# Three chunk loads of 16 rows a partition become two loads of 24 rows in a row-softmax kernel

## Chip, cores and metric

The kernel runs on one core of a Trainium2 chip. The metric is the device time of one execution in microseconds, the median of several runs.

## What is computed

A softmax with temperature 0.5 over the last dimension of a float32 tensor of shape (16, 1024, 512), that is 16384 rows of 512 values:

```python
x_scaled = x / 0.5
x_max = np.max(x_scaled, axis=-1, keepdims=True)
exp_x = np.exp(x_scaled - x_max)
out = exp_x / np.sum(exp_x, axis=-1, keepdims=True)
```

Each row is on its own. Input and output are 33.55 MB each.

## The kernel before

**Tiling.** The rows are cut into C = 8 chunks of 128 x 16 rows, numbered 0 to 7 here (the change's "fourth to sixth" are chunks 3, 4 and 5). In a chunk each of the 128 partitions holds G = 16 rows that lie one after the other in HBM, so a partition's share is one run of 16 x 512 x 4 bytes = 32 KiB. `LOADS` (L38) says how a chunk's rows are split over DMAs: chunk 0 in 4 and 12 rows, chunks 1 to 6 whole, chunk 7 without its last row, which `load_last_row` brings later in two small DMAs of GpSimd. There are six chunk buffers (`BUFS`, L42); chunks 6 and 7 take the buffers of chunks 0 and 1 and so wait until those are stored.

**Blocks.** Work goes by blocks (`BLOCKS`, L39): chunk 0 is three blocks (4, 4 and 8 rows), chunks 1 to 6 are one block each, chunk 7 two of 8 rows. For a block

- `shift` issues the chunk's load when nobody has yet (L66, on the SP queue), takes the negated maximum of each row with one VectorE reduction (L74) and doubles it to a bias (L78);
- `exponentials` runs one ScalarE activation per row, exp(2x + bias), in place, and sums the row in the same instruction (L103);
- `scale_vector` takes reciprocals of the sums (L120) and multiplies seven eighths of the rows on VectorE (L122); `scale_scalar` multiplies the rest on ScalarE (L131);
- `store` sends the whole chunk once its last block is done (L139, on ScalarE's DMA queue, 16 rows a partition).

**Order.** The order of instructions on each engine is the order of the program text (L143 to L161); no scheduler moves them. VectorE thus alternates: scale block i, maxima of block i + 2, scale block i + 1, and so on. Each engine runs its list in order, so an instruction that waits holds up all that stands behind it on that engine. The SP queue holds the loads in the order of the chunks. The first seven load DMAs (chunks 0 to 5) wait for nothing and are issued in the first 4 us; those of chunks 6 and 7 wait for the stores of chunks 0 and 1. Stores go out through the other queue (q10 in the profile; the loads are q1). Both queues are worked off by the same 16 DMA engines.

Of the kernel before, what the change touches and what calls it, by code (L numbers as in the profile page):

```python
# [1 line left out]

# [4 lines left out]


@with_exitstack
def kernel(  # L10
    ctx: ExitStack,
    tc: tile.TileContext,
    x: bass.AP,
    out: bass.AP,
):
    nc = tc.nc
    fp32 = mybir.dt.float32
    P = nc.NUM_PARTITIONS
    AX = mybir.AxisListType.X
    EXP = mybir.ActivationFunctionType.Exp  # L20
    COPY = mybir.ActivationFunctionType.Copy
    MAX = mybir.AluOpType.max

    D = x.shape[-1]
    xf = x.flatten_outer_dims()
    of = out.flatten_outer_dims()
    N = xf.shape[0]

    G = 16
    C = N // (P * G)
    assert C * P * G == N
    xr = xf.rearrange("(c p g) d -> c p g d", p=P, g=G)
    outr = of.rearrange("(c p g) d -> c p g d", p=P, g=G)
    WHOLE = [(0, G)]
    LOADS = [[(0, 4), (4, G)]] + [WHOLE] * 6 + [[(0, G - 1)]]  # L38
    BLOCKS = [[(0, 4), (4, 8), (8, G)]] + [WHOLE] * 6 + [[(0, 8), (8, G)]]  # L39
    STORES = [WHOLE] * 8  # L40
    BMAX = 16
    BUFS = 6  # L42

    data = ctx.enter_context(tc.tile_pool(name="data", bufs=BUFS))
    stats = ctx.enter_context(tc.tile_pool(name="stats", bufs=6))

    ctx.enter_context(tc.manual_schedule())


    warm = stats.tile([P, 1], fp32, name="warm", bufs=1)  # L50
    nc.vector.memset(warm, 0.0)  # L51
    nc.scalar.activation(out=warm, in_=warm, func=EXP)  # L52

    chunks = {}
    blocks = [(c, lo, hi) for c in range(C) for lo, hi in BLOCKS[c]]
    n = len(blocks)
    biases, sums, recips = {}, {}, {}

    def load(c):
        if c < BUFS:  # L60
            chunks[c] = data.tile([P, G, D], fp32, name="xt")
        else:
            chunks[c] = chunks[c - BUFS]
        xt = chunks[c]
        for lo, hi in LOADS[c]:
            nc.sync.dma_start(out=xt[:, lo:hi, :], in_=xr[c][:, lo:hi, :])  # L66

    def shift(i):
        c, lo, hi = blocks[i]
        if c not in chunks:  # L70
            load(c)
        b = hi - lo
        negmax = stats.tile([P, BMAX], fp32, name="negmax")
        nc.vector.tensor_reduce(  # L74
            negmax[:, 0:b], chunks[c][:, lo:hi, :], axis=AX, op=MAX, negate=True
        )
        biases[i] = stats.tile([P, BMAX], fp32, name="bias")
        nc.vector.tensor_scalar_mul(biases[i][:, 0:b], negmax[:, 0:b], 2.0)  # L78

    def load_last_row(signal):
        seen = stats.tile([P, 1], fp32, name="seen", bufs=1)
        nc.gpsimd.tensor_copy(out=seen, in_=signal)  # L87
        c = C - 1
        halves = "p (h d) -> p h d"
        to = chunks[c - BUFS][:, G - 1, :].rearrange(halves, h=2)  # L90
        of_ = xr[c][:, G - 1, :].rearrange(halves, h=2)
        for p0, p1 in ((P - 2, P), (0, P - 2)):
            nc.gpsimd.dma_start(  # L93
                out=to[p0:p1], in_=of_[p0:p1], max_dma_last_dim=2 * D
            )

    def exponentials(i, rows):
        c, lo, hi = blocks[i]
        if i not in sums:
            sums[i] = stats.tile([P, BMAX], fp32, name="sums")  # L100
        for g in rows:
            row = chunks[c][:, lo + g, :]
            nc.scalar.activation(  # L103
                out=row,
                in_=row,
                func=EXP,
                bias=biases[i][:, g : g + 1],
                scale=2.0,
                accum_out=sums[i][:, g : g + 1],
            )  # L110
            if c == BUFS - 1 and g == 10:
                load_last_row(sums[i][:, g : g + 1])


    def scale_vector(i):
        c, lo, hi = blocks[i]
        b = hi - lo
        k = b - b // 8
        recips[i] = stats.tile([P, BMAX], fp32, name="recip")
        nc.vector.reciprocal(recips[i][:, 0:b], sums[i][:, 0:b])  # L120
        rows = chunks[c][:, lo : lo + k, :]
        nc.vector.tensor_mul(  # L122
            rows, rows, recips[i][:, 0:k].unsqueeze(2).broadcast_to((P, k, D))
        )

    def scale_scalar(i):
        c, lo, hi = blocks[i]
        b = hi - lo
        for g in range(b - b // 8, b):
            row = chunks[c][:, lo + g, :]  # L130
            nc.scalar.activation(  # L131
                out=row, in_=row, func=COPY, scale=recips[i][:, g : g + 1]
            )

    def store(i):
        c, _, end = blocks[i]
        for lo, hi in STORES[c]:
            if hi == end:
                nc.scalar.dma_start(  # L139
                    out=outr[c][:, lo:hi, :], in_=chunks[c][:, lo:hi, :]  # L140
                )

    shift(0)  # L143
    shift(1)

    def rows(i):
        c, lo, hi = blocks[i]
        cut = hi - lo - (2 if c == 1 else 0)
        return range(cut), range(cut, hi - lo)

    exponentials(0, rows(0)[0])
    for i in range(n):
        if i + 1 < n:
            exponentials(i + 1, rows(i + 1)[0])
        scale_vector(i)
        scale_scalar(i)
        if i + 2 < n:
            shift(i + 2)
        store(i)
        if i + 1 < n:  # L160
            exponentials(i + 1, rows(i + 1)[1])  # L161


# [1 line left out]
_INS = ['x']  # L165
_OUTS = [((16, 1024, 512), 'float32')]


# [23 lines left out]
```

## Time and profile before

The median of 3 runs is 162.08 us (161.99 to 162.23); the profiled execution has a span of 160.3 us on the core.

| engine | busy us | share of span | instructions |
|---|---|---|---|
| VectorE (DVE) | 134.6 | 84% | 45 |
| ScalarE (ACT) | 102.2 | 64% | 273 |
| GpSimd (POOL) | 1.9 | 1% | 7 |

| work | count | mean ns of one |
|---|---|---|
| row maxima of 16 rows, L74 | 6 | 8679 |
| scaling of 14 rows on VectorE, L122 | 6 | 7626 |
| exponential of one row, L103 | 128 | 708 (and 187 to read the sum) |
| load of a whole chunk, 4096 KB, L66 | 6 | 34.8 us from issue to landing (median) |
| store of a chunk, 4096 KB, L139 | 8 | 22.7 us from issue to landing (median) |

How to read it: TensorE is not used. The page's line "DMA" gives, for 40 equal slices of the span, the mean busy share of the 16 DMA engines in tenths (9 is 90% or more). Its chain is the work that ended last, followed back from the last instruction, in shares of the span. A line of the waits reads "engine and line <- what it waited for: us in total, times, longest us". A line of the timeline starts with the start and the duration in us. A line of the DMA view for a queue gives packets, MB and the time that the packets took, as a share of 16 engines over the stretch asked for; a line for an issue gives the number of issues, KB each and the median us from issue to landing. The trace also keeps each DMA packet with queue, size, start and duration.

### The profile page before, as it was taken

To read this page: it belongs to the slowest core of one execution; us is meant where nothing else is said; L and a number is where in the kernel's file an instruction comes from. 1 tells how busy PE (TensorE), PEld (TensorE's weight loads), DVE (VectorE), ACT (ScalarE), POOL (GpSimd) and SP (SyncE) were. 2 spreads that over 40 slices of the span, in tenths; PEclk is the share of its full clock that TensorE was granted. 3 is DMA by queue.
4 is the path that set the end of the run, shared out by engine and by line. 5 is a ranking of instruction groups with operands and counts; after the bars stand their busy time and mean duration, and the time that the engine had idled before them with its cause. 6 is when DMAs were issued, how large, how long until landed. Compare 5 with 4: busy or idle time off the path is not lost.

```text
span 160.3 us, 410 instructions
## 1 busy us (share of the span) xinstructions
DVE 134.6 (84%) x45; ACT 102.2 (64%) x273; POOL 1.9 (1%) x7
## 2 busy tenths in 40 slices
DVE  0608999999999999999999999999999999957000
ACT  3071549069989963998199909991899891790000
POOL 0000000000000000000000000030000000000000
DMA  5999999999999999999999989999999999999993
GB/s 180 474 393 523 393 393 507 409 393 452 458 393 401 393 393 515 401 393 491 425 393 466 450 385 470 415 422 462 421 437 401 450 458 401 425 474 401 401 507 139
DMA packets 2578, 67.13 MB, mean 419 GB/s; under 512 B 328, under 2 KB 328, under 8 KB 400
## 3 DMA queue, kind: packets, MB, share of 16 engines
q1 hardware_dynamic: 1296, 33.29, 49.1%
q10 hardware_dynamic: 1152, 33.55, 48.5%
q0 software_dynamic: 128, 0.26, 0.4%
q14 instruction: 2, 0.02, 0.0%
HBM read 33.55 MB, written 33.55 MB: 419 GB/s over the span
## 4 chain that ended last, share of the span: by engine, by line
DVE 75%; DMA 7%; issue 5%; ACT 3%; SPq 0%
DVE negmax L74 42%; DVE xt L122 32%; DMA xt<-in_x_dram 7%; ACT xt L103 3%; DVE bias L78 1%; DVE recip L120 1%; SPq L66 0%
## 5 line engine op out<-in xcount | busy, mean ns | idle before, releaser
L103 ACT ACTIVATE xt<-xt,bias 128x512 f32<-128x512 f32 x128 | 90.4, 708 | 41.4 <-DVE bias L78 40.5
L74 DVE TENSOR_REDUCE negmax<-xt 128x16 f32<-128x8192 f32 (+2 forms) x11 | 69.9, 6352 | 9.4 <-DMA xt<-in_x_dram 9.4
L122 DVE TENSOR_TENSOR xt<-xt,recip 128x7168 f32<-128x7168 f32 (+2 forms) x11 | 62.0, 5637 | 0.4
L103 ACT ACTIVATION_READ_ACCUMULATOR xt<-xt,bias 128x1 f32 x128 | 23.9, 187 | 0.0
L131 ACT ACTIVATE xt<-xt,recip 128x512 f32<-128x512 f32 x15 | 9.9, 706 | 0.0
L120 DVE RECIPROCAL recip<-sums 128x16 f32<-128x16 f32 (+2 forms) x11 | 2.4, 218 | 1.8 <-ACT xt L103 1.8
L78 DVE TENSOR_SCALAR bias<-negmax 128x16 f32<-128x16 f32 (+2 forms) x11 | 1.9, 173 | 0.4
L52 ACT ACT_TABLE_LOAD x1 | 1.3, 1283 | 0.7 <-PEq L176 0.7
L93 POOL DMA_DIRECT2D xt<-in_x_dram x2 | 1.5, 741 | 0.5 <-issue 0.5
L87 POOL COPY seen<-sums 128x1 f32<-128x1 f32 x1 | 0.2, 183 | 103.6 <-ACT xt L103 103.6
L51 DVE MEMSET warm<- 128x1 f32 x1 | 0.1, 59 | 0.8 <-PEq L176 0.8
L52 ACT ACTIVATE warm<-warm 128x1 f32<-128x1 f32 x1 | 0.2, 203 | 0.0
L176 POOL MEMSET const-float32-0.0<- 128x1 f32 x1 | 0.1, 93 | 0.2 <-issue 0.2
L176 POOL MEMSET const-bfloat16-1.0<- 128x1 bf16 x1 | 0.1, 95 | 0.0
L176 POOL MEMSET const-uint8-127<- 128x1 uint8 x1 | 0.1, 95 | 0.0
L176 POOL MEMSET const-float32-1.0<- 128x1 f32 x1 | 0.1, 93 | 0.0
## 6 DMA issues: line engine op xcount, KB each, us to landing
out_dram<-xt ACTq DMA_DIRECT2D x8, 4096.0 KB, 22.7
xt<-in_x_dram SPq DMA_DIRECT2D x6, 4096.0 KB, 34.8
xt<-in_x_dram SPq DMA_DIRECT2D x1, 3840.0 KB, 28.1
xt<-in_x_dram SPq DMA_DIRECT2D x1, 3072.0 KB, 11.5
xt<-in_x_dram SPq DMA_DIRECT2D x1, 1024.0 KB, 4.7
xt<-in_x_dram POOLq DMA_DIRECT2D x1, 252.0 KB, 15.2
xt<-in_x_dram POOLq DMA_DIRECT2D x1, 4.0 KB, 8.7
```

What stands on the lines that cost most here:

```text
L51: nc.vector.memset(warm, 0.0)
L52: nc.scalar.activation(out=warm, in_=warm, func=EXP)
L74: nc.vector.tensor_reduce(negmax[:, 0:b], chunks[c][:, lo:hi, :], axis=AX, op=MAX, negate=True)
L78: nc.vector.tensor_scalar_mul(biases[i][:, 0:b], negmax[:, 0:b], 2.0)
L87: nc.gpsimd.tensor_copy(out=seen, in_=signal)
L93: nc.gpsimd.dma_start(out=to[p0:p1], in_=of_[p0:p1], max_dma_last_dim=2 * D)
L103: nc.scalar.activation(out=row, in_=row, func=EXP, bias=biases[i][:, g : g + 1], scale=2.0, accum_out=sums[i][:, g : g + 1],)
L120: nc.vector.reciprocal(recips[i][:, 0:b], sums[i][:, 0:b])
L122: nc.vector.tensor_mul(rows, rows, recips[i][:, 0:k].unsqueeze(2).broadcast_to((P, k, D)))
L131: nc.scalar.activation(out=row, in_=row, func=COPY, scale=recips[i][:, g : g + 1])
L176: nc = _bacc.Bacc("TRN2", target_bir_lowering=False, num_devices=1)
```

## The change

Chunks 3, 4 and 5 become one group of 48 rows a partition. They lie in one buffer of three times the size, and in HBM a partition now owns 48 consecutive rows (96 KiB) of the group's 6144, where before it owned three separate runs of 16. The group is loaded by two DMAs of 24 rows each, so a partition's run per DMA is 48 KiB instead of 32 KiB, and there are two DMAs and two landings instead of three. A load is issued as far as the rows of the wanted chunk need it: before chunk 3's maxima the first, before chunk 4's the second, before chunk 5's none. The maxima of chunk 3 wait for the first load; those of chunk 4 take rows 16 to 31 and so wait for both; those of chunk 5 need nothing more. The aim is larger pieces for the DMA engines and fewer transfers.

Blocks, computing instructions, their order on each engine, and the stores (still one of 16 rows a partition for each chunk, 32 KiB pieces) are as before; a store's pieces for chunks 3 to 5 now lie 96 KiB apart in HBM instead of side by side. The buffers take the same memory.

```diff
+    GROUPS = [(0,), (1,), (2,), (3, 4, 5), (6,), (7,)]
-    WHOLE = [(0, G)]
-    LOADS = [[(0, 4), (4, G)]] + [WHOLE] * 6 + [[(0, G - 1)]]
-    STORES = [WHOLE] * 8
+    LOADS = [
+        [(0, 4), (4, G)],
+        [(0, G)],
+        [(0, G)],
+        [(0, 24), (24, 48)],
+        [(0, G)],
+        [(0, G - 1)],
+    ]
...
+    chunks, group_of, waiting = {}, {}, {}
+    for k, members in enumerate(GROUPS):
+        first, m = members[0], len(members)
+        hbm = slice(first * P * G, (first + m) * P * G)
+        into = xf[hbm].rearrange("(p g) d -> p g d", p=P)
+        back = of[hbm].rearrange("(p g) d -> p g d", p=P)
+        if first < BUFS:
+            xt = data.tile([P, m * G, D], fp32, name=f"xt{k}")
+        else:
+            xt = group_of[first - BUFS][0]
+        for at, c in enumerate(members):
+            group_of[c] = (xt, into, back, k, at * G)
+            chunks[c] = xt[:, at * G : (at + 1) * G, :]
+        waiting[k] = list(LOADS[k])
...
     def load(c):
-        xt = chunks[c]
-        for lo, hi in LOADS[c]:
-            nc.sync.dma_start(out=xt[:, lo:hi, :], in_=xr[c][:, lo:hi, :])
+        xt, into, _, k, at = group_of[c]
+        while waiting[k] and waiting[k][0][0] < at + G:
+            lo, hi = waiting[k].pop(0)
+            nc.sync.dma_start(out=xt[:, lo:hi, :], in_=into[:, lo:hi, :])
```

## The prediction

> Chunks are numbered 0 to 7. The two new loads are A (rows 0 to 23 of the long partition runs: all of chunk 3, half of chunk 4) and B (rows 24 to 47: the rest of chunk 4, all of chunk 5). Times in the trace are from the span's start; the measured time, 162.08 us, is 1.8 us more than the span.
>
> **What bounds the kernel now.** I read the page first: its slices and its chain.
>
> ```profile
> DMA  5999999999999999999999989999999999999993
> DMA packets 2578, 67.13 MB, mean 419 GB/s; under 512 B 328, under 2 KB 328, under 8 KB 400
> q1 hardware_dynamic: 1296, 33.29, 49.1%
> q10 hardware_dynamic: 1152, 33.55, 48.5%
> DVE 75%; DMA 7%; issue 5%; ACT 3%; SPq 0%
> ```
>
> Two things are full at once. The 16 DMA engines are busy from the first slice to the last: loads (q1) and stores (q10) take 97.6% of their time. And the chain that ended last is VectorE. The waits say how much air VectorE has:
>
> ```profile
> DVE negmax L74 <- DMA xt<-in_x_dram: 9.4, 2, 4.8
> DVE recip L120 <- ACT xt L103: 1.8, 1, 1.8
> ```
>
> It waits twice for chunk 0 at the start, once for ScalarE at the end, and nowhere between: from 12.7 to 141.4 us it runs without a gap, so a delay there goes through to its end undiminished. The timeline at the end shows how the two limits meet:
>
> ```profile
> 143.44 3.89 DVE L122 TENSOR_TENSOR xt<-xt,recip 128x3584 f32<-128x3584 f32 x1
> 147.42 0.34 ACTq L139 DMA_DIRECT2D out_dram<-xt  x1
> ```
>
> The last store is issued at 147.42 us. In the packet records its first pieces start at 148.63 to 148.98 us on most engines, at once after the store before it, so the engines don't idle. The first load needed 1.02 us from issue (0.74) to its first piece (1.76), so this store could have started at about 148.44. VectorE's tail therefore has 0.2 to 0.5 us of slack against the DMA engines; I take 0.3.
>
> Then the loads that change, by asking the DMA view for one issue each (chunks 3, 4 and 5, issued at 2.76, 3.26 and 3.79 us; they land at 42.3, 57.3 and 76.7 us), and what VectorE needs them for:
>
> ```profile
> xt<-in_x_dram SPq DMA_DIRECT2D x1, 4096.0 KB, 39.6
> ```
> ```profile
> xt<-in_x_dram SPq DMA_DIRECT2D x1, 4096.0 KB, 54.1
> ```
> ```profile
> xt<-in_x_dram SPq DMA_DIRECT2D x1, 4096.0 KB, 72.9
> ```
> ```profile
> 53.94 8.68 DVE L74 TENSOR_REDUCE negmax<-xt 128x16 f32<-128x8192 f32 x1
> 63.02 7.62 DVE L122 TENSOR_TENSOR xt<-xt,recip 128x7168 f32<-128x7168 f32 x1
> 70.56 8.68 DVE L74 TENSOR_REDUCE negmax<-xt 128x16 f32<-128x8192 f32 x1
> ```
>
> The maxima of chunk 3 start at 53.94, of chunk 4 at 70.56, of chunk 5 at 87.18 us. Before the change the slack is 11.6, 13.2 and 10.5 us. Chunk 4's is the one to watch: it will need B as well.
>
> Last, how loads and stores share the engines. From 17 to 41 us only loads run; from 58 to 66 us both do:
>
> ```profile
> q1 hardware_dynamic: 347, 10.32, 99.7%
> ```
> ```profile
> q10 hardware_dynamic: 50, 1.64, 47.4%
> q1 hardware_dynamic: 49, 1.61, 46.4%
> ```
>
> 10.32 MB are 315 pieces of 32 KiB: 0.997 x 16 x 24 / 315 = 1.215 us each. With both queues filled the pieces alternate one for one. The packet records give 0.309, 0.912, 1.138 and 1.213 us for pieces of 8, 24, 30 and 32 KiB: 0.0368 ns a byte plus 7.5 ns, hence an estimated 1.816 us for 48 KiB.
>
> **What the Trainium skill says.** "DMA: Bandwidth & Descriptors", section "Queues, rings and completion order": an engine takes its queues in turn, packet by packet. The trace agrees (49 against 50). Same page, "Why a DMA increments its semaphore by 16 and not by 1": 128 partitions are spread over 16 engines, each engine's last descriptor is its part of the signal, one descriptor moves one contiguous run, and only the full 16 means landed. The trace agrees: 9 loads left 1296 packets, which is 9 x (128 + 16), and the slowest engine sets a landing (chunk 4: fifteen engines by 55.96, the last at 57.34). Its "Where 436 GB/s comes from" puts the ceiling at 435 GB/s; here 32 KiB in 1.213 us on 16 engines is 432. Bigger pieces can't go past it.
>
> **The change part by part.** *Removed:* 128 of 384 load pieces and one DMA. 128 x 7.5 ns / 16 = 0.06 us of engine time, and one of nine signals. Bytes, engines' instructions and stores are the same. VectorE, ScalarE and GpSimd keep their order; ScalarE's wait for B moves into the middle of chunk 4's exponentials, behind VectorE's own wait for it. SP issues two DMAs for three within its first 4 us, hidden behind chunk 0's load. These cost nothing.
>
> *Chunk 3 waits for A.* A starts where chunk 3's load did: chunk 2's pieces end at 31.4 to 31.7 us in the records. 8 pieces x 1.816 = 14.53, so A ends at about 46.1 and lands (0.35 us later, as the other loads do) by 46.5, some 47 on the slowest engine. Needed at 53.94: hidden by chunk 2's maxima and chunk 1's scaling.
>
> *Chunk 4 waits for B.* Only this can reach the end. B starts at about 46.1, and its 8 pieces take 14.53. Chunk 0's store, issued at 44.02, alternates with them, so the question is how many store pieces come before B's signal. In the trace of before, the piece in hand about 1.0 to 1.5 us after that issue was followed by two more load pieces before the first store piece (49.3 to 49.5 us), and the signal takes a turn of its own (the order at 54 to 56 us is: eighth load piece, store piece, signal, store piece). After the change the piece in hand is A's last; I let the two turns be A's signal and B's first piece. Then a store piece follows each of B's 8: 8 x 1.213 = 9.70. In this first meeting of the queues the load pieces also ran longer, 1.6 to 1.8 us in place of 1.213, for one or two pieces: 0.4 to 0.85 us, I take 0.6. Sum: 46.1 + 14.53 + 9.70 + 0.6 + 0.35 = 71.3 us on most engines. One engine was 0.46 us behind at chunk 3 (42.33 against 41.87); with it B lands at 71.8. The same sum for chunk 4 before, 41.3 + 9.71 + 3 x 1.213 + 0.85 + 0.35 = 55.9, meets its 55.7 to 55.96.
>
> So VectorE waits 71.8 - 70.56 = 1.2 us. Queued behind this reduce are chunk 4's bias, which ScalarE's exponentials need, the scaling of chunk 3 with its store, and all later work of VectorE; nothing takes the delay up before the last store. That is issued 1.2 us later; with 0.3 us of slack the end moves by 0.9 us. Less the 0.06: 162.08 + 0.9 = **163.0 us**. Bounds: one meeting piece fewer or more and no slack or 0.5 us of it give +0.5 to +1.6.
>
> *Later loads.* Chunk 6's load waits for chunk 0's store, which, getting 40% of the time beside 48 KiB pieces and not 50%, lands at about 71.7 instead of 68.1. q1 then stands empty for 3 to 4 us, but q10 still holds chunk 1's store, issued at 58.9, so the engines stay busy. Chunk 6 then lands at about 96 us and is needed at 105; it costs nothing.
>
> **Rivals.** (a) *The early switch goes the other way*: the two turns are B's first two pieces. One store piece fewer precedes the signal; B lands at 71.8 - 1.2 = 70.6 if the lagging engine follows suit, 71.0 if it meets the longer pieces. The wait is 0.1 to 0.5, the end moves by 0 to 0.2: 162.2 us. For it: whether a 4-byte signal uses up a place in that look-ahead isn't seen in the trace. Against: it does take a turn.
> (b) *Restarting the load queue costs engine time.* When q10 first joined, the engines lost 0.85 us; q1 restarting after its empty stretch could lose as much. DMA engines being full, all stores shift by 0.85: the end is the later of this and VectorE's delay, so 162.9, or 163.4 with longer 48 KiB pieces in the first meeting. Against it: q0, joining at 110 us, cost nothing visible.
> (c) *Faster.* If the first meeting loses nothing, the DMA engines finish up to 0.85 us earlier and B is in time. But the last store still waits for VectorE's 147.42 and could start at 148.44: at most 0.5 us, 161.7. Nothing in the change shortens VectorE's stretch.
> (d) *The 48 KiB pieces don't alternate as wholes*: cut in two halves of 24 KiB, or turns counted in bytes. By bytes, loads get half of the time, and B takes 14.5 + 13.5 and lands near 75: 166 us. As halves, 16 pieces x (0.91 + 1.21) put B near 80: 170 us. The trace shows whole runs of up to 32 KiB as one packet, nothing longer.
>
> **How the numbers follow.** Main case 0.50, (a) 0.25, (b) 0.12, (c) 0.05, (d) 0.08. Within 0.2% (0.32 us) fall most of (a) and the edge of the main case: 0.26. Faster is (c) alone: 0.05. Slower is the rest: 0.69. The range leaves out (c)'s lower end, (d), and little else: 162.0 to 163.9.
>
> **What would show it.** Right: a third wait of VectorE's maxima for the load, about 1.2 us, at 70.6 us; B landing 68 us after its issue; q1 with 1152 packets; alternate pieces of 48 and 32 KiB; the last store issued at 148.6; DMA slices still full. Wrong if no such wait appears (a), if VectorE waits but the end does not move, so that the slack was larger, if packets lengthen or pause near 72 to 76 us (b), or if q1 keeps 1296 packets or more (d).

## The result and the profile after

The changed kernel takes 164.03 us (163.94 to 164.33), the kernel before beside it 162.06 us (161.99 to 162.23): ratio 1.0123, 95% interval 1.0106 to 1.0141, or 1.97 us slower. The forecast was slower, 163.0 us, with a range that ended at 163.9. The direction was right; the size was half of what came. Executions more than 1.5% above the fastest of their kernel are left out of every time and ratio here: three of 21 of the second held load below and two of five of the run with four loads of 12 rows, whose only trace is of such an execution and is not read.

The page of the changed kernel, its line of DMA slices, its packets and its two large queues:

```profile
DMA  5999899989989999999999999999999999999993
DMA packets 2434, 67.13 MB, mean 414 GB/s; under 512 B 312, under 2 KB 312, under 8 KB 384
q1 hardware_dynamic: 1152, 33.29, 49.0%
q10 hardware_dynamic: 1152, 33.55, 48.4%
```

The loads have 1152 packets instead of 1296, as 8 loads of 128 + 16 must have: each run of 48 KiB is one packet. The engines are as full as before, yet move 414 GB/s instead of 419.

VectorE's waits, then its timeline at chunk 4's maxima, and the second long load (B), asked for by its issue at 3.29 us:

```profile
DVE negmax L90 <- DMA xt<-in_x_dram: 10.8, 3, 4.8
```
```profile
62.96 7.63 DVE L138 TENSOR_TENSOR xt<-xt,recip 128x7168 f32<-128x7168 f32 x1
72.04 8.69 DVE L90 TENSOR_REDUCE negmax<-xt 128x16 f32<-128x8192 f32 x1 [1.45 <-DMA xt<-in_x_dram]
```
```profile
xt<-in_x_dram SPq DMA_DIRECT2D x1, 6144.0 KB, 68.7
```

There is the third wait, 1.45 us (1.2 was forecast), and B lands at 72.0 (71.8 was forecast). It stays with VectorE to the end: the last store is issued at 148.91 us instead of 147.42.

```profile
148.91 0.34 ACTq L155 DMA_DIRECT2D out_dram<-xt  x1
```

So far the main case holds. But now the last two stores, first before and then after, again by their issues (KB, then us from issue to landing; the upper line of each pair is the last but one):

```profile
out_dram<-xt ACTq DMA_DIRECT2D x1, 4096.0 KB, 16.5
out_dram<-xt ACTq DMA_DIRECT2D x1, 4096.0 KB, 11.7
```
```profile
out_dram<-xt ACTq DMA_DIRECT2D x1, 4096.0 KB, 17.2
out_dram<-xt ACTq DMA_DIRECT2D x1, 4096.0 KB, 12.4
```

The last but one is issued at 134.43 us and lands at 151.6 (149.5 before); the last needs 12.4 us instead of 11.7 on top of VectorE's delay. If VectorE's lateness alone set the end, the engines would have stood free for the last store, and it would have needed less time, not more. The DMA engines are late as well. Two stretches show where they lose time; first before, then after (the last three columns are granted clock, DMA share and GB/s):

```profile
74.00:78.00 4.00, 4.00 (x1) 1.48 (x4) 0.00 (x0) 1.00 0.91 393
84.00:88.00 4.00, 4.00 (x2) 4.00 (x13) 0.00 (x0) 1.00 0.93 401
```
```profile
74.00:78.00 4.00, 4.00 (x1) 1.42 (x4) 0.00 (x0) 1.00 0.99 352
84.00:88.00 4.00, 4.00 (x1) 4.00 (x12) 0.00 (x0) 1.00 1.04 360
```

A packet counts where it starts, so short stretches waver; what matters is the pair of columns. Before, share and rate go together (0.91 with 393, that is 432 at a share of 1). After, a share of about 1 moves only 350 to 360: the packets are there, but they take longer. The packet records show which pieces these are, against the price of 0.0368 ns a byte plus 7.5 ns of the prediction:

- The first meeting of the queues costs 0.80 us an engine, as before the change (0.84).
- From 48.5 to 60.7 us, where pieces of 48 and 32 KiB alternate, not one in this trace is longer than its price by over 0.05 us. From 60.8 to 67.3 us 18 store pieces are, by up to 0.35 us.
- From 75.2 to 76.4 us 16 store pieces, the last ones ahead of chunk 6's first load piece (76.8 us), take 1.5 to 2.1 us instead of 1.213; 7 load pieces up to 78.4 us take 1.3 to 1.9.
- From 84.5 to 86.8 us, just ahead of the end of chunk 1's store, 24 of chunk 6's load pieces take 1.3 to 2.3 us.

The last two groups make up about 1.55 of some 1.7 us that an engine loses on average after the first meeting, and their pieces are of 32 KiB on both queues. So the loss hardly falls where the long pieces alternate with the short; it comes after that. Over the whole middle, before and after:

```profile
50.00:146.00 96.00, 93.76 (x27) 73.26 (x196) 1.66 (x3) 1.00 1.00 432
```
```profile
50.00:146.00 96.00, 92.31 (x27) 73.20 (x196) 1.67 (x3) 1.00 0.99 421
```

11 of 432 GB/s over 96 us are some 2.4 us of work left over at 146 us. The sum of all packet times, divided by 16 engines, grew from 157.22 to 158.74 us, although 128 pieces fewer were moved.

### The profile page after: what moved, and what is told of

Same layout as the page of the kernel before. It is cut to its first block, busy times and chain, and to the rows that moved or that the text cites. A ratio compares the mean times of both kernels' runs of the same rounds, so it can differ in the third digit from the quotient of the medians.

```text
span 162.2 us, 407 instructions
## 1 busy us (share of the span) xinstructions
DVE 134.7 (83%) x45; ACT 102.2 (63%) x273; POOL 1.9 (1%) x7
## 3 DMA queue, kind: packets, MB, share of 16 engines
q1 hardware_dynamic: 1152, 33.29, 49.0%
q10 hardware_dynamic: 1152, 33.55, 48.4%
## 4 chain that ended last, share of the span: by engine, by line
DVE 75%; DMA 7%; issue 5%; ACT 3%; another core or an unknown queue 1%; SPq 0%
DVE negmax L90 41%; DVE xt L138 31%; DMA xt<-in_x_dram 7%; ACT xt L119 3%; DVE bias L94 1%; DVE recip L136 1%; SPq L83 0%
```

## The experiments

Two causes were then on the table: V, VectorE's wait; and D, time lost by the DMA engines. For D there were three candidates in turn: a queue that runs empty and restarts (rival (b) of the prediction), pieces of a certain size, and pieces of different length on the two queues.

**The layout alone.** The group of 48 rows, loaded in three DMAs.

```diff
-        [(0, 24), (24, 48)],
+        [(0, 16), (16, 32), (32, 48)],
```

> The changed kernel with the group of 48 rows a partition kept, but loaded in three DMAs of 16 rows (pieces of 32 KiB, three landings). If the new layout in HBM (runs 96 KiB apart for loads and stores) matters, some of the 1.97 us stays. Both theories (VectorE's wait for the second load; engine time lost when a DMA queue restarts) say that it does not: 162.1 us, no wait of VectorE at 70.6 us, queue q1 never empty before 113 us.

Measured: 162.16 us beside 162.10 before, ratio 1.0007 (1.0001 to 1.0014), and 432 GB/s from 50 to 146 us. The new layout costs nothing worth the name; all of the 1.97 us is in how the loads are cut.

**The changed kernel without VectorE's wait.**

```diff
-        nc.vector.tensor_reduce(
-            negmax[:, 0:b], chunks[c][:, lo:hi, :], axis=AX, op=MAX, negate=True
-        )
+        parts = [(0, 8), (8, 16)] if c == 4 else [(0, b)]
+        for p, q in parts:
+            nc.vector.tensor_reduce(
+                negmax[:, p:q], chunks[c][:, lo + p : lo + q, :],
+                axis=AX, op=MAX, negate=True,
+            )
```

> The changed kernel with chunk 4's maxima taken in two reductions of 8 rows; the first needs only the first long load, the second starts at about 75 us, after the second long load (72.0) has landed. VectorE's wait of 1.43 us goes and 0.1 us is added. Theory V (VectorE's wait alone set the end): back to 162.1 to 162.4 us. Theory D (time that the DMA engines lost, 1.5 us more of packet time than before the change, sets the end whatever VectorE does): 163.3 to 164.0 us, with the lengthened packets at 74 to 78 and 84 to 88 us still there.

Measured: 164.47 us (164.23 to 165.12), ratio 1.0156 (1.0140 to 1.0172). Its timeline and its last two stores (issued at 132.97 and 147.45 us):

```profile
63.00 7.62 DVE L141 TENSOR_TENSOR xt<-xt,recip 128x7168 f32<-128x7168 f32 x1
70.54 8.74 DVE L92 TENSOR_REDUCE negmax<-xt 128x8 f32<-128x4096 f32 x2
```
```profile
out_dram<-xt ACTq DMA_DIRECT2D x1, 4096.0 KB, 18.9
out_dram<-xt ACTq DMA_DIRECT2D x1, 4096.0 KB, 14.1
```

VectorE doesn't wait, and the last store is issued when it was before the change, but it needs 14.1 us instead of 11.7. From 50 to 146 us the engines move 422 GB/s:

```profile
50.00:146.00 96.00, 93.77 (x28) 73.23 (x196) 1.66 (x3) 1.00 1.00 422
```

Theory V as the whole cause has fallen: the engines' lost time is enough by itself. (That it comes out 0.4 us above the changed kernel is not explained; in its trace one engine finishes chunk 0's store at 73.3, where the slowest of the changed kernel does at 72.2.)

**VectorE's delay alone.** The kernel before with a spare reduction.

```diff
+        if c == 4:
+            spare = stats.tile([P, 5], fp32, name="spare", bufs=1)
+            nc.vector.tensor_reduce(
+                spare, chunks[c][:, 0:5, 0:256], axis=AX, op=MAX, negate=True
+            )
```

> The kernel before with a spare VectorE reduction of 1280 values a partition put ahead of chunk 4's maxima: VectorE is 1.42 us later from 70.6 us on, the DMAs are those of before. Theory V with the predicted slack of 0.3 us: 163.2 us; with no slack, 163.5. Theory D alone (VectorE's delay is absorbed): 162.1 us. If V is the whole of the change's cost, 164.0.

Measured: 163.20 us (163.15 to 163.27), ratio 1.0073 (1.0060 to 1.0086): 1.1 us for 1.42 us of delay, as the predicted slack of 0.3 us has it. The last store and the stretch in front of its pieces:

```profile
out_dram<-xt ACTq DMA_DIRECT2D x1, 4096.0 KB, 11.1
```
```profile
147.00:150.50 3.50, 1.76 (x1) 0.00 (x0) 0.00 (x0) 1.00 0.70 300
```

Here the engines do stand idle for the late store (share 0.70), and it lands 11.1 us after its issue. So V is real and was sized rightly; in the changed kernel it is covered by the larger delay of the engines. The two don't add up: the last store starts when both are ready.

**A restart of the load queue alone.** The kernel before, chunk 6's load held by a late read of the buffer that it overwrites.

```diff
+            if c == 3 and g == 15:
+                held = stats.tile([P, 1], fp32, name="held", bufs=1)
+                nc.scalar.activation(out=held, in_=chunks[0][:, 0, 0:1], func=COPY)
```

> The kernel before, with the load of chunk 6 held until about 74 us by a one-column ScalarE copy out of chunk 0's buffer behind chunk 3's last exponential. Queue q1 runs empty at 75 us and restarts beside a full store queue, with 32 KiB pieces and no wait of VectorE. Theory D: packets lengthen for about 2 us around 76 to 79 us, 0.7 us of engine time is lost (1.5 if the second lengthening at 84 to 88 us comes with it), and the end moves by as much: 162.8 to 163.6 us. Theory V: chunk 6 lands at about 98 us, is needed at 104, and the time stays 162.1.

Measured: 162.23 us median, ratio 1.0018 (1.0008 to 1.0028). The load was issued at 74.6 us, its first pieces started at 78.2, and but for four load pieces (1.3 to 1.4 us) the packets keep their 1.213 us:

```profile
74.00:78.00 4.00, 4.00 (x1) 1.82 (x5) 0.00 (x0) 1.00 0.93 401
84.00:88.00 4.00, 4.00 (x2) 4.00 (x12) 0.00 (x0) 1.00 0.98 418
```

The expected 0.7 us didn't come in the median, nor in the traced execution (162.18 us). But 6 of the 22 executions took 162.79 to 163.22 us, where none of the 41 of the kernel before passed 162.46; none of the six was traced, so what they lost time on stays open. A second version made sure that the queue was empty on every engine when the load was issued:

```diff
         store(i)
+        if blocks[i][0] == 2:
+            held = stats.tile([P, D], fp32, name="held", bufs=1)
+            for _ in range(2):
+                nc.scalar.activation(out=held, in_=chunks[0][:, 0, :], func=COPY)
```

> The kernel before with chunk 6's load held until about 77 us by two spare ScalarE copies out of chunk 0's buffer behind chunk 2's store, so that q1 is empty on all engines when the load is issued (in the run held to 74.6 us it had emptied within the same half microsecond, and nothing was lost in its profile). D-idle with emptiness at the issue as the cause: packets lengthen ahead of chunk 6's first pieces, 0.7 to 1.6 us lost, 162.8 to 163.7 us. D-pieces: 162.1 to 162.3.

Measured: 162.54 us (162.16 to 163.38), ratio 1.0025 (1.0015 to 1.0035), and 431 GB/s at a share of 1.00 from 75 to 82 us. In its profile VectorE waits 0.32 us for chunk 7, most of what the median moved (0.42 us). No piece from 70 to 90 us is longer than its price by over 0.05 us, while in the changed kernel, whose q1 had run empty too, 16 store pieces ahead of chunk 6's first were. In the two traces the restart costs the engines nothing visible, and the two medians move by 0.1 and 0.4 us: an empty queue alone does not bring the 2 us, so rival (b)'s cause has fallen too.

**A queue kept from running empty.** The changed kernel with a thin load behind B, as it is and with the two half reductions.

```diff
             nc.sync.dma_start(out=xt[:, lo:hi, :], in_=into[:, lo:hi, :])
+        if c == 4:
+            thin = stats.tile([P, 32], fp32, name="thin", bufs=1)
+            nc.sync.dma_start(out=thin, in_=xf[0:P, 0:32])
```

> The changed kernel with one thin extra load (128 bytes a partition, into a spare tile) queued on q1 behind the second long load. Its 8 tiny pieces take about 0.1 us in all, but one turn each, so q1 stays filled from 71 to about 81 us and chunk 6's load joins a queue that is not empty. Theory D-idle (the packets lengthen because q1 had run empty): the lengthened packets at 74 to 78 and 84 to 88 us go, VectorE's wait of 1.4 us stays, 163.2 us as with the VectorE delay alone. Theory D-pieces (the pieces of 48 KiB themselves throw the engines out of step): still 164.0.

> The changed kernel with both taken away: chunk 4's maxima in two halves (no wait of VectorE) and the thin load behind the second long load (q1 never empty). D-idle: 162.1 to 162.4 us, the time before the change. D-pieces: 164.0 to 164.5, as with the halves alone.

Measured: 163.78 (163.49 to 164.23) and 164.42 us (163.84 to 165.16); ratios 1.0102 (1.0085 to 1.0118) and 1.0138 (1.0115 to 1.0160). As times these two decide nothing: the thin load also puts chunks 6 and 7 back, and with the halves VectorE now waits for chunk 7.

```profile
122.57 4.42 DVE L95 TENSOR_REDUCE negmax<-xt 128x8 f32<-128x4096 f32 x1 [1.84 <-DMA xt<-in_x_dram]
```

What they do show is that the lengthened packets need no empty queue. In the run without the halves chunk 6's load, issued at 72.5 us, joined a queue that held the thin pieces until 81 us, and the stretch of its joining is again full and slow:

```profile
78.00:84.00 6.00, 5.93 (x4) 2.84 (x9) 0.00 (x0) 1.00 0.97 361
```

**Other cuts of the group.** In these three chunk 4's rows land before VectorE needs them at 70.6 us, by the sums that were made ahead of the runs, and q1 still holds pieces when chunk 6's load is due:

```diff
-        [(0, 24), (24, 48)],
+        [(0, 16), (16, 40), (40, 48)],
```

> The group of 48 rows loaded in three DMAs of 16, 24 and 8 rows: pieces of 32, 48 and 16 KiB. The 48 KiB pieces meet chunk 0's store, the second load lands at about 63 us (VectorE needs it at 70.6), and q1 still holds 16 KiB pieces when chunk 0's store lands at about 68.5. D-idle: no wait of VectorE, no empty queue, 162.1 to 162.3 us. D-pieces: lengthened packets and 163 us or more.

```diff
+        [(0, 16), (16, 36), (36, 48)],
```

> The group of 48 rows in DMAs of 16, 20 and 12 rows: pieces of 32, 40 and 24 KiB; the 40 KiB pieces meet chunk 0's store, no wait of VectorE and no empty q1 are due. D-size with a loss that grows with the piece: between 162.1 and the 164.1 us of the run with 32, 48 and 16 KiB, about 163. D-size with a step above 32 KiB: 164. If 48 KiB or the final 16 KiB pieces alone are bad: 162.1 to 162.3.

```diff
+        [(0, 12), (12, 24), (24, 36), (36, 48)],
```

> The group of 48 rows loaded in four DMAs of 12 rows (pieces of 24 KiB against the stores' 32 KiB); by the sums, each chunk lands before VectorE needs it and q1 is never empty before chunk 6's load joins. If any mismatch between the load's and the store's piece makes the engines lose time (D-mismatch): 163 us or more. If only pieces above 32 KiB do (D-size): 162.1 to 162.3 us.

Measured: 164.10 us (163.19 to 164.61), 163.56 us (163.08 to 164.13) and 164.36 us (164.00 to 164.90); ratios 1.0104 (1.0085 to 1.0123), 1.0087 (1.0066 to 1.0108) and 1.0143 (1.0122 to 1.0163). The last one is the telling one: its pieces are *smaller* than the stores'. A loss needs no piece above 32 KiB. What the engines did in those executions was not traced.

In the first two VectorE waits for no load but chunk 0's. The run with 32, 48 and 16 KiB:

```profile
DVE negmax L90 <- DMA xt<-in_x_dram: 9.4, 2, 4.8
```
```profile
out_dram<-xt ACTq DMA_DIRECT2D x1, 4096.0 KB, 19.1
out_dram<-xt ACTq DMA_DIRECT2D x1, 4096.0 KB, 14.3
```

Both stores are issued within 0.01 us of their times before the change, and land 2.6 us later. Yet 50 to 146 us reads 432 GB/s:

```profile
50.00:146.00 96.00, 93.77 (x27) 73.25 (x196) 1.67 (x3) 1.00 1.00 432
```

The loss has another shape here: fifteen engines keep time, and one falls behind. The signals of the last store but one arrive from 148.48 to 149.34 us on fifteen engines and at 152.06 on the last (before: from 148.41 to 149.48 on all sixteen). A rate over 16 engines can hardly show that, but every landing waits for the slowest one. (In the kernel before, one engine's signals of chunks 4 to 7 come 1.4 to 2.0 us behind the others' on the load queue, but none is behind on the store queue.) In the run with 40 KiB it is the same: 149.6 for fifteen, 151.27 for the last. In the changed kernel no single engine is far behind; the signals of this store spread from 149.51 to 151.58.

**The changed kernel once more.**

> The changed kernel once more, unaltered, beside the runs that follow from it. If the engine time lost at about 74 to 78 and 84 to 88 us is what sets its end, both stretches show again fewer GB/s at a DMA share near 1.0, and the time is 163.9 to 164.5. If they were chance in one execution, they are elsewhere or gone, and VectorE's wait of 1.4 us alone leaves 163.2.

Measured: 164.17 us (164.00 to 164.29), ratio 1.0126 (1.0113 to 1.0139), 422 GB/s from 50 to 146 us; the lengthened packets come at 74 to 78 and 84 to 88 us as before. They are no chance of one execution.

**Equal pieces of another size.** If it is the inequality, then cutting both queues to 16 KiB must be harmless but for the number of pieces. (The first half of most stores also goes out some 4 us earlier than the whole store did.)

```diff
-    LOADS = [[(0, 4), (4, G)]] + [WHOLE] * 6 + [[(0, G - 1)]]
+    HALVES = [(0, 8), (8, G)]
+    LOADS = [[(0, 4), (4, G)]] + [WHOLE] * 2 + [HALVES] * 4 + [[(0, 8), (8, G - 1)]]
...
-    STORES = [WHOLE] * 8
+    STORES = [HALVES] * 8
...
-            if hi == end:
+            if end == G:
```

> The kernel before with every store, and every load from chunk 3 on, cut into two DMAs of 8 rows (the last load of 8 and 7): nearly all pieces that meet are 16 KiB, equal on both queues, but not 32 KiB. It has 1664 more pieces, which at 7.5 ns each over 16 engines are 0.8 us. D-mismatch (engines lose time when the pieces of the two queues differ in length): no engine falls behind, 162.8 to 163.0 us. If any piece other than 32 KiB is bad (D-not-32): one engine or all fall behind as in the runs with 24, 40 or 48 KiB, 164 us or more. More DMAs share the semaphores, so a store may wait a little for an earlier one; the profile must show that nothing else waits.

Measured: 163.03 us (162.86 to 163.12) beside 162.25 before, ratio 1.0051 (1.0037 to 1.0065). Its packets and its middle stretch:

```profile
DMA packets 4450, 67.13 MB, mean 417 GB/s; under 512 B 536, under 2 KB 536, under 8 KB 608
```
```profile
50.00:146.00 96.00, 93.77 (x27) 73.41 (x197) 1.67 (x3) 1.00 1.01 431
```

0.8 us for 1664 more pieces is what an estimated 7.5 ns for each come to on 16 engines. After 48 us a single packet is lengthened (0.85 us instead of 0.61), no engine falls behind, and VectorE waits for nothing new. The kernel before points the same way for a small difference: in it chunk 7's 30 KiB pieces alternate with 32 KiB ones from 95 to 113 us, one of them lengthened, and no engine is late on the store queue.

| run | load pieces that meet stores, KiB | store pieces, KiB | us |
|---|---|---|---|
| before | 32 | 32 | 162.1 |
| three loads in the new layout | 32 | 32 | 162.16 |
| all in halves | 16 | 16 | 163.03, of which 0.8 for the number |
| 16, 20 and 12 rows | 40, then 24 | 32 | 163.56 |
| 16, 24 and 8 rows | 48, then 16 | 32 | 164.10 |
| four of 12 rows | 24 | 32 | 164.36 |
| the change | 48 | 32 | 164.03, 164.17 |
| the change without VectorE's wait | 48 | 32 | 164.47 |

These runs show that the cuts with unequal pieces cost time and those with equal ones do not: the layout alone brought no loss, and with VectorE's wait, the empty queue or the sizes above 32 KiB taken away it stayed. Two things were not separated. Unequal pieces also give the two queues unequal shares of the engines, and so move the places where loads and stores join; and only the loads were cut unequal, never the stores. *Why* it costs time is open. The traces show when packets lengthen (at the joining of chunk 6's load, at the change from one store to the next, and hardly while the unequal pieces alternate), and in the runs with 48 and 40 KiB pieces in the middle that an engine once behind on the store queue stays behind to the end; what in the engines or in the memories makes it so is not seen, and no run here tells it.

## Why the prediction was wrong in size

- *B lands at 71.8, VectorE waits 1.2 us:* held; 72.02 and 1.45, in the repeat 72.11 and 1.47. The last signal was met in part by luck, as two terms of the sum were off in opposite ways: the first meeting took 0.80 us and not 0.6, and no single engine was 0.46 us behind the others; their signals spread from 71.16 to 72.02. The disputed look-ahead went as chosen: in the packet records A's last piece is followed by its signal, B's first piece and only then, at 48.5 us, a store piece. Rival (a) is out.
- *The slack of the tail is 0.3 us, so the end moves by 0.9:* held as a statement on VectorE alone. The spare reduction gave 1.1 us for 1.42. With the measured wait the same sum would have been about 163.2.
- *"Later loads ... it costs nothing", because q10 keeps the engines busy:* this step failed. Busy is not the same as fast. The engines had packets all the time, and spent 1.5 us more each on average on 128 pieces fewer; the last store landed 2.1 us later. But for the first meeting all pieces were priced with 1.213 and 1.816 us wherever they stand. In these runs that sum came out only where the pieces of both queues were equal or nearly so; here 16 store pieces ahead of chunk 6's load took up to 2.1 us, and 24 load pieces ten us later up to 2.3.
- *Rival (b)* had the place right (the joining of chunk 6's load) and the cause wrong. It blamed the empty queue and allowed one loss of 0.85 us with a chance of 0.12. A restart with equal pieces cost nothing in the two traces and 0.1 and 0.4 us in the medians; the loss was nearly twice the 0.85, with no empty queue needed.
- *(c) and (d)* didn't occur: nothing became faster, and 48 KiB runs do alternate as wholes.
- *Range:* it joined VectorE's bounds with one restart. A resource in use for 97.6% of the span, with 0.3 us to spare against VectorE, deserved a term for its own efficiency under a new mix of pieces. There was none, so 163.9 was too low.

## What to carry to other kernels

Where a load and a store stream share DMA engines that are full, start from equal pieces on both and measure any other cut; here longer pieces saved an estimated 0.06 us of fixed cost and lost about 2 us. A merged transfer lands as one, so look for the first consumer that needs its last part, and weigh that wait against the slack at the end. And when two resources meet at the end with little slack, the later of the two sets the time: test each cause by itself, for removing one may change nothing.

## What the runs showed of the hardware that was not expected

- 32 KiB against 32, 16 against 16 and 32 against 30 KiB alternate at 431 to 432 GB/s; kernels with 24, 40 or 48 KiB load pieces beside 32 KiB store pieces took 1.4 to 2.4 us longer. Where the traces show the loss as lengthened pieces, most of it falls after the unequal pieces, on pieces of 32 KiB.
- DMA share and rate can part: share 0.99 to 1.04 with 352 to 360 GB/s where 432 is normal. A line of full slices doesn't show it; the rate in a stretch does.
- One engine of sixteen can be 2.7 us late while the other fifteen and the mean rate (432 GB/s) look as before. Only the arrival of the last signal tells.
- A 4-byte signal takes a turn between the queues like a large piece: in the kernel before, chunk 4's signals start at 55.3 to 55.6 us, one store piece after its last load piece, and the next store piece follows each.
